# A planned MLP stage that starts four weight tiles earlier and names its buffers

## The chip, the cores and the metric

The kernel runs on one core of a Trainium2 chip, in one launch. The metric is the device time of that launch in microseconds (us), and the median of three runs is taken. TensorE (PE) multiplies matrices; its weight loads (PEld) are listed apart. VectorE (DVE) and ScalarE (ACT) do element-wise work, GpSimd (POOL) a little more of it and the transfers that it issues itself, and SyncE (SP) issues the weight loads from the chip's main memory.

## The reference

A two-layer transformer trunk in fp32, for 256 tokens of width 2048. Each layer adds to the residual stream an attention block (12 main heads and 4 heads that look at 256 memory tokens) and then an MLP:

```python
def sq_relu_mlp(h, g, w_in, w_out):
    return jnp.square(jax.nn.relu(rms_norm(h, g) @ w_in)) @ w_out

def reference(...):
    h = x
    for layer in range(DEPTH):
        ...
        h = h + jnp.concatenate([y_main, y_mem], axis=-1) @ w_o[layer]
        h = h + sq_relu_mlp(h, norm_mlp[layer], w_mlp_in[layer], w_mlp_out[layer])
    return h
```

The MLP's hidden width is 8192, so each layer has two weight matrices of 2048 x 8192. They are most of the work, and all that the change is about lies in or around them.

## The kernel before, in words

**Arithmetic.** Every fp32 weight is split into two parts of the type fp32r: `hi`, a rounded copy, and `lo`, what the rounding lost. A *unit* is one weight block of 128 x 1024. SP loads it (512 KB), ACT casts it to `hi`, DVE subtracts to make `lo`. A product takes hi x hi, hi x lo and lo x hi.

**The up half.** An up tile (`U`, one of 64 per layer) is 128 hidden features for all 256 tokens. It takes two units: 16 matmuls of 512 columns (hi weights against both parts of the activations) and 16 of 256 columns (lo weights). ACT then copies the low half of the bank (`low`), DVE adds the halves (`up`), DVE multiplies `relu` by the token norm (`ri_mlp`, made by `inverse_root`), ACT squares, and the result is split into `hid`. `after_up` lists these operations.

**The down half.** The hidden width is cut into four chunks (`c`) of 16 up tiles. For each chunk the output is done in two halves (`n`). A step `S` is a Strassen-like step with seven products instead of eight: 21 matmuls of 512 columns, from two loads. DVE makes four sums of weight blocks (512 columns each), and ACT and DVE split four units out of the two loads. For each pair of up tiles `block_ops` makes the sums of activations that such a step needs. Steps `A` and `B` are plain products of 12 matmuls. Sums of a chunk leave over POOL's queue to main memory, with an add on the way for later chunks, and come back in the last chunk.

**The order.** `mlp_steps` gives TensorE's order: two tiles done by halves (`H`), pairs of tiles (`T`), single tiles (`U`), then turns of `U` and `S`, and `A`, `B` at a group's end. The `H` and `T` steps run in the plain way: `weights()` prepares at most four units ahead in the pools `raw` (6 buffers), `hi` (4) and `lo` (5), and side work such as `inverse_root` or `finish` is run a given number of *slots* (half a pair of tiles, say) later. In the kernel before the plain way covers tiles 0 to 7, and `up` runs `after_up` at once for tiles 4 to 7 and at fixed slots for tiles 0 to 3.

From tile 8 on (L1450 and after) each engine's order is written out by a planner, `in_turn` (L106). It keeps a clock per engine with fixed costs (`CAST`, `SUM`, `WIDE`), a list of free 128 x 1024 buffers and counts of smaller tiles, and starts a job when its inputs are told and its buffers free. Here the pool `g4` (8 of 9 buffers) joins the 15 of the plain way, so 23 in all, and any of them may hold a load, a `hi` or a `lo`. TensorE, POOL and SP take their jobs in the order given; ACT and DVE take the first of 160 by due time (`key`) that can start. A load starts only if `RESERVE` buffers stay free beside its own. The resulting order is kept by every engine. In the kernel before, the planner chooses a kind and a number, but the tile is then asked of the pool by its kind alone (`slot_tile`, L1450), and the pool gives whichever of its buffers it takes.

The clock of the planner begins at zero for all engines when the `H` and `T` steps have been written.

**After the plan.** The last output tiles come from plain code: four more units are loaded within the plan (`tail_units`), the stored sums are merged (`merged`, `merge_first`), turned by transposes (`turned`), and in the last layer the last four tiles go through `down` and `last_tile`, where GpSimd adds the residual, and are stored.

Everything outside the MLP (projections, attention, output projection) uses the plain way. The pool `g4` holds the heads there, also with buffers that the pool picks.

Of the kernel before, what the change touches and what calls it, by code (L numbers as in the profile page):

```python
# [10 lines left out]
F32 = mybir.dt.float32  # L11
# [28 lines left out]
COPIES, SPARE, HORIZON, SUMS, FROM, LATE, RESERVE, URGENT = 4, 8, 12000, 4800, 5, -7, 3, 3000  # L40
# [51 lines left out]
SOON = 200  # L92


class Job:


    def __init__(self, engine, cost, emit, key, after=(), take=0, give=(), get=(), free=(), adds=False, kinds="g4 raw hi lo"):
# [4 lines left out]
        self.slots, self.tiles, self.kinds = [], [], kinds.split()  # L103


def in_turn(jobs, slots, counts, reserve=RESERVE):  # L106
# [5 lines left out]
    ready = {e: 0 for e in queues}  # L112
# [7 lines left out]
    def fits(job, now):  # L120
        kinds = job.kinds
        if job.engine != "POOL" and (q := queues["POOL"]) and q[0].take and ripe(q[0], now):
            kinds = [x for x in kinds if x != "g4"]
        return [x for x in slots if x[0] in kinds]

    def can(job, now):
# [4 lines left out]
        if job.take and len(fits(job, now)) < job.take + (  # L131
            reserve if job.engine == "SP" else 0
# [4 lines left out]
    while events:  # L137
# [6 lines left out]
        while again:  # L144
            again = False
            for e, queue in queues.items():
# [10 lines left out]
                queue.remove(job)  # L157
# [7 lines left out]
                for _ in range(job.take):  # L165
                    job.slots.append(fits(job, now)[0])
                    slots.remove(job.slots[-1])
# [13 lines left out]
    return order  # L181
# [51 lines left out]
def trunk(  # L233
# [20 lines left out]
    raws = ctx.enter_context(tc.tile_pool(name="raws", bufs=6))  # L254
    his = ctx.enter_context(tc.tile_pool(name="his", bufs=4))
    los = ctx.enter_context(tc.tile_pool(name="los", bufs=5))
    acts = ctx.enter_context(tc.tile_pool(name="acts", bufs=2))
    grp = ctx.enter_context(tc.tile_pool(name="grp", bufs=9))
# [46 lines left out]

    def prepare_pair(load, split):
# [7 lines left out]
                raws.tile([P, 1024], F32, name=f"raw{n}", tag="raw"),  # L314
                his.tile([P, 1024], F32R, name=f"hi{n}", tag="hi"),
                los.tile([P, 1024], F32R, name=f"lo{n}", tag="lo"),
# [15 lines left out]
    def prepare_seven(i, seven):  # L332

        if seven.step == 0:
            seven.raw = []
            for n, ap in enumerate(seven.sides):
                raw = raws.tile([P, 1024], F32, name=f"raw{i}_{n}", tag="raw")
                nc.sync.dma_start(raw[:].rearrange("p (o x) -> p o x", o=4), ap)
                seven.raw.append(raw[:].rearrange("p (o k n) -> p k o n", o=4, k=2))
        left, right = seven.raw  # L340
        b11, b21, b12, b22 = left[:, 0], left[:, 1], right[:, 0], right[:, 1]
        hi = his.tile([P, 1024], F32R, name=f"hi{i}", tag="hi")
        lo = los.tile([P, 1024], F32R, name=f"lo{i}", tag="lo")
        hi4 = hi[:].rearrange("p (k o n) -> p k o n", o=4, k=2)
        lo4 = lo[:].rearrange("p (k o n) -> p k o n", o=4, k=2)
        src = left if seven.step in (0, 3) else right
        if seven.step == 1:
            src, hi4, lo4 = b22, hi4[:, 0], lo4[:, 0]
        elif seven.step == 2:
            nc.vector.tensor_tensor(b22, b22, b12, op=ALU.subtract)  # L350
# [1718 lines left out]
```

## Time and profile before

| what | value |
|---|---|
| runs of the kernel before | 2185.88 us median of 3 (2182.7 to 2189.06) |
| the profiled execution | 2179.71 us, span 2177.9 us, granted clock 0.998 |
| PE busy | 2144.5 us, 98% of the span |
| DVE busy | 1803.9 us, 83% |
| ACT busy | 1308.2 us, 60% |
| POOL busy | 259.7 us, 12% |
| MLP of the first layer, from tile 8 to the end of the plan | about 480 to 1080 us of the span |
| MLP of the second layer, the same | about 1520 to 2120 us |

The profile page gives the busy time of each engine, the span in 40 slices, and the chain of work that ended last. Views of the trace give, for a stretch of the span, each engine's busy time (so idle time is the length less the busy time), the single instructions in order of time with the idle time before them, and the waits. A matmul of 512 columns is listed with some 390 ns, but the next one starts some 227 ns after it: they overlap, and a short stall hides in part in that overlap.

### The profile page before, as it was taken

What the parts mean: (1) busy time and instruction counts of PE and PEld (TensorE: products, weight loads), DVE (VectorE), ACT (ScalarE), POOL (GpSimd) and SP (SyncE); (2) the same over time, 40 slices, a digit from 0 to 9 for tenths busy, and PEclk for the clock granted to TensorE, in tenths of its full rate; (3) what the DMA queues carried; (4) which work ended last, traced back from release to release, by engine and by line L of the source; (5) the groups of instructions that cost most, each with busy time, mean ns of one, the idle gap of its engine ahead of it and who ended that gap; (6) DMA issues with size and microseconds to landing.
All of it is one profiled execution on the core that took longest, in us unless ns stands there. A gap on an engine that the chain in (4) does not pass through costs nothing.

```text
span 2177.9 us, 30420 instructions
## 1 busy us (share of the span) xinstructions
PE 2144.5 (98%) x10966; PEld 1827.2 (84%) x10966; DVE 1803.9 (83%) x2745; ACT 1308.2 (60%) x1968; POOL 259.7 (12%) x307
## 2 busy tenths in 40 slices
PE   9999999999999999999999999999999999999998
PEld 8888888887888888888878888888788888888887
DVE  7778885679999899999785556567999989899985
ACT  7644545556766666666445447555766666676652
POOL 0110112610000000001050112361000000000100
PEclk9999999999999999999999999999999999999999
DMA  9655556675767768769666564467576776886973
GB/s 328 214 162 187 167 182 206 211 245 155 239 210 243 202 196 243 229 199 314 216 188 211 186 191 129 140 214 232 169 231 191 251 212 199 250 233 202 289 245 114
DMA packets 225415, 458.71 MB, mean 211 GB/s; under 512 B 14576, under 2 KB 145648, under 8 KB 225264
## 3 DMA queue, kind: packets, MB, share of 16 engines
q1 hardware_dynamic: 212592, 410.63, 59.7%
q0 software_dynamic: 12096, 44.05, 7.3%
q10 hardware_dynamic: 576, 2.10, 0.3%
q8 instruction: 86, 1.41, 0.3%
q14 instruction: 65, 0.53, 0.1%
HBM read 424.21 MB, written 32.51 MB: 210 GB/s over the span
## 4 chain that ended last, share of the span: by engine, by line
PE 77%; DVE 14%; DMA 5%; issue 3%; ACT 1%; SPq 0%; DVEq 0%; ACTq 0%
PE acc L194 73%; DVE g4s L194 4%; DVE raws L194 2%; DVE los L194 2%; DVE his L194 2%; DMA his<-in_w_down 2%; DMA raws<-in_w_down 1%; PE accs L194 1%; PE yp L194 1%; DVE up L194 1%; DMA los<-in_w_down 1%; DMA g4s<-in_w_down 1%; PE tp L194 1%; PE s L194 1%; PE z L194 1%
## 5 line engine op out<-in xcount | busy, mean ns | idle before, releaser
L304 DVE TENSOR_TENSOR lo<-raw,hi 128x1024 fp32r<-128x1024 f32 (+1 forms) x308 | 382.7, 1251 | 180.1 <-ACT hi L301 153.0
L301 ACT CAST hi<-raw 128x1024 fp32r<-128x1024 f32 (+2 forms) x308 | 318.8, 1039 | 274.2 <-PE acc L194 228.0
L194 PE MATMUL acc<-hi,xg 128*128 128x512 f32 x640 | 208.4, 398 | 0.0
L194 PE MATMUL acc<-mlpx,g4s 128*128 128x256 f32 (+1 forms) x1024 | 190.1, 333 | 0.0
L194 PE MATMUL acc<-mlpx,raws 128*128 128x512 f32 (+1 forms) x960 | 183.2, 336 | 2.0 <-DVE up L194 2.0
L194 PEld LDWEIGHTS acc<-mlpx,g4s 128*128 128x128 f32 x1024 | 161.4, 190 | 21.4
L194 PE MATMUL acc<-g4s,hid 128*128 128x512 f32 x504 | 173.9, 392 | 1.4 <-DVE hid L194 1.1
L194 PEld LDWEIGHTS acc<-mlpx,raws 128*128 128x128 f32 x960 | 153.3, 189 | 24.3 <-DVE up L194 3.2
L194 PE MATMUL acc<-raws,hid 128*128 128x512 f32 x430 | 150.8, 394 | 2.2 <-DVE hid L194 1.3
L194 PE MATMUL acc<-mlpx,los 128*128 128x512 f32 (+1 forms) x720 | 146.7, 350 | 0.0
L194 PEld LDWEIGHTS acc<-hi,xg 128*128 128x128 f32 x640 | 120.2, 188 | 24.7
L194 PE MATMUL acc<-mlpx,his 128*128 128x256 f32 (+1 forms) x752 | 137.6, 328 | 2.6 <-DVE up L194 2.6
L194 PEld LDWEIGHTS acc<-mlpx,los 128*128 128x128 f32 x720 | 120.1, 190 | 18.9
L194 PE MATMUL acc<-los,hid 128*128 128x512 f32 x358 | 129.9, 395 | 4.6 <-DVE los L194 4.4
L194 PEld LDWEIGHTS acc<-mlpx,his 128*128 128x128 f32 x752 | 116.8, 190 | 18.2 <-DVE up L194 3.7
L194 POOL DMA_DIRECT2D e<-copy x24 | 18.2, 760 | 946.2 <-ACT copy L194 942.8
L194 PE MATMUL acc<-lo,xg 128*128 128x512 f32 x320 | 124.8, 390 | 0.6 <-DVE lo L304 0.6
L194 PE MATMUL acc<-y,hi 128*128 128x512 f32 x512 | 119.9, 391 | 0.0
L194 PE MATMUL acc<-his,hid 128*128 128x512 f32 x334 | 115.9, 397 | 0.0
L194 PEld LDWEIGHTS acc<-g4s,hid 128*128 128x128 f32 x504 | 94.0, 188 | 20.8 <-DVE hid L194 2.0
L194 PEld LDWEIGHTS acc<-y,hi 128*128 128x128 f32 x512 | 95.0, 188 | 19.1
L194 ACT ACTIVATE up<-up 128x256 f32<-128x256 f32 x112 | 46.8, 417 | 91.1 <-DVE up L194 90.6
(351 smaller groups left out, 4910.8 us busy)
## 6 DMA issues: line engine op xcount, KB each, us to landing
raw<-in_w_in SPq DMA_DIRECT2D x80, 512.0 KB, 4.1
g4s<-in_w_up SPq DMA_DIRECT2D x76, 512.0 KB, 9.1
g4s<-in_w_down SPq DMA_DIRECT2D x75, 512.0 KB, 8.7
los<-in_w_down SPq DMA_DIRECT2D x72, 512.0 KB, 7.8
raw<-in_w_o SPq DMA_DIRECT2D x64, 512.0 KB, 4.1
raws<-in_w_up SPq DMA_DIRECT2D x58, 512.0 KB, 9.0
raws<-in_w_down SPq DMA_DIRECT2D x53, 512.0 KB, 9.1
los<-in_w_up SPq DMA_DIRECT2D x50, 512.0 KB, 6.7
```

The costliest lines, as they stand in the source:

```text
L194: return self._tc.keep_in_program_order(fn(*args, **kwargs))
L301: nc.scalar.copy(hi[:, :n], raw[:, :n])
L304: nc.vector.tensor_tensor(lo, raw, hi.bitcast(F32), op=ALU.subtract)
```

## The change

The plan starts after one pair step instead of three, so it holds up tiles 4 to 8 and the `after_up` work of tiles 0 to 3 too. Each of the 23 buffers is a tile tag of its own with one buffer, and a job writes exactly the buffer that the planner took; the same is done for the heads in `g4` and for the plain units, which go round in order. `RESERVE` goes from 3 to 4 and counts all free buffers, ACT and DVE are taken to be 1500 ns busy when the plan starts, and the four units loaded for after the plan take one `raw`, one `hi` and one `lo` buffer each instead of any of the three. `inverse_root` starts one slot earlier. In the last layer DVE makes the residual adds of output tiles 14 and 15, which GpSimd made before. The last two pieces of the memory tokens are loaded in program order. A branch for seven-product units in the plain way, which nothing used, is removed.

```diff
+PLANNED = 4
-COPIES, SPARE, HORIZON, SUMS, FROM, LATE, RESERVE, URGENT = 4, 8, 12000, 4800, 5, -7, 3, 3000
+COPIES, SPARE, HORIZON, SUMS, FROM, LATE, RESERVE, URGENT, EARLY = 4, 8, 12000, 4800, 5, -7, 4, 3000, 1500
...
-SOON = 200
+SOON, BACKLOG = 200, 1500
...
 def mlp_steps(l):
     steps = [(0, 0, "H", 0)]
-    steps += [(0, 0, "T", f) for f in range(FIRST_UP, ALONE - 1, 2)]
-    steps += [(0, 0, "U", f) for f in range(ALONE - ALONE % 2, ALONE)]
+    steps += [(0, 0, "T", f) for f in range(FIRST_UP, PLANNED, 2)]
+    steps += [(0, 0, "U", f) for f in range(PLANNED, ALONE)]
...
-    ready = {e: 0 for e in queues}
+    ready = {e: BACKLOG if e in OVERLAP else 0 for e in queues}
...
     def fits(job, now):
-        kinds = job.kinds
-        if job.engine != "POOL" and (q := queues["POOL"]) and q[0].take and ripe(q[0], now):
-            kinds = [x for x in kinds if x != "g4"]
-        return [x for x in slots if x[0] in kinds]
+        queue = queues["POOL"]
+        kept = job.engine != "POOL" and queue and queue[0].take and ripe(queue[0], now)
+        found = []
+        for kinds in job.take:
+            slot_ = next(
+                (x for x in slots if x[0] in kinds and x not in found and not (kept and x[0] == "g4")), None
+            )
+            if slot_ is None:
+                return None
+            found.append(slot_)
+        return found
...
-        if job.take and len(fits(job, now)) < job.take + (
-            reserve if job.engine == "SP" else 0
+        if job.take and (
+            fits(job, now) is None or job.engine == "SP" and len(slots) < len(job.take) + reserve
         ):
...
+    pools = {"raw": raws, "hi": his, "lo": los, "g4": grp}
+    turns = {"raw": deque(range(6)), "hi": deque(range(4)), "lo": deque(range(5))}
+
+    def buffer(kind, m, dtype, name):
+        return pools[kind].tile([P, 1024], dtype, name=name, tag=f"{kind}{m}")
+
+    def next_of(kind, dtype, name):
+        turns[kind].rotate(-1)
+        return buffer(kind, turns[kind][-1], dtype, name)
...
-    def heads4(name):
-        return grp.tile([P, 1024], F32, name=name, tag="g4")
+    def heads4(name, m):
+        return buffer("g4", m, F32, name)
...
     def mlp(l, xg_, sq, h, done):
-        start_side(delayed(inverse_root(sq, f"mlp{l}"), 4))
+        start_side(delayed(inverse_root(sq, f"mlp{l}"), 3))
...
         def up(c, f, bank):
-            early = c == 0 and f < 4
-            add_up(c, f, bank, low_part(bank), early)
-            if early:
-                later(lambda: finish(c, f), began + 11 + f - clock["slot"])
-            else:
-                finish(c, f)
-
+            add_up(c, f, bank, low_part(bank), True)
...
-                job.tiles.append(pools[kind].tile([P, 1024], dtype, name=f"{kind}s{l}_{m}", tag=kind))
+                job.tiles.append(buffer(kind, m, dtype, f"{kind}s{l}_{m}"))
...
+        for f in range(PLANNED):
+            ready_at[0, f] = chain(
+                after_up(0, f), EARLY * f + 1500, None, ready_at[0, f - 1] if f % 2 else ()
+            )
+            if f % 2:
+                held[0, f // 2] = [x for job in ready_at[0, f] for x in job.get if x in ("wide", "bias")]
...
         for m in range(AHEAD + 1):
-            tail_units.append(flat_unit(at, begins[-1] + 1500 * m, "raw hi lo"))
+            tail_units.append(flat_unit(at, begins[-1] + 1500 * m, (("raw",), ("hi",), ("lo",))))
...
-            nc.gpsimd.tensor_tensor(h(o), h(o), t[:], op=ALU.add)
+            (nc.vector if l == 1 and o >= KT - 2 else nc.gpsimd).tensor_tensor(h(o), h(o), t[:], op=ALU.add)
             done(o)
 
         def down_early(o, bank):
             low = low_part(bank)
-            nc.gpsimd.tensor_tensor(low[:], low[:], h(o), op=ALU.add)
+            nc.vector.tensor_tensor(low[:], low[:], h(o), op=ALU.add)
             nc.vector.tensor_tensor(h(o), bank[:, :T], low[:], op=ALU.add)
...
-    qm = heads4("qm0")
+    qm = heads4("qm0", 8)
...
-        q_, k_, v_ = heads4(f"q{i}"), heads4(f"k{i}"), heads4(f"v{i}")
+        q_, k_, v_ = (heads4(f"{x}{i}", m) for x, m in zip("qkv", ((0, 1, 2), (3, 6, 7), (0, 1, 2))[i]))
```

More of the change, by code (lines that the diff above doesn't have):

```diff
@@ L91, with __init__ @@
 LANDS, MOVES, ADDS = 3400, 1690, 2600
-SOON = 200
+SOON, BACKLOG = 200, 1500
 class Job:
-    def __init__(self, engine, cost, emit, key, after=(), take=0, give=(), get=(), free=(), adds=False, kinds="g4 raw hi lo"):
+    def __init__(self, engine, cost, emit, key, after=(), take=(), give=(), get=(), free=(), adds=False):
         self.engine, self.cost, self.emit, self.key = engine, cost, emit, key
@@ L164, in in_turn @@
                     counts[c] -= 1
-                for _ in range(job.take):
-                    job.slots.append(fits(job, now)[0])
-                    slots.remove(job.slots[-1])
+                job.slots = fits(job, now)
+                for x in job.slots:
+                    slots.remove(x)
+                queue.remove(job)
                 if e in ("SP", "POOL"):
@@ L313, in prepare_pair @@
                 stream[n],
-                raws.tile([P, 1024], F32, name=f"raw{n}", tag="raw"),
-                his.tile([P, 1024], F32R, name=f"hi{n}", tag="hi"),
-                los.tile([P, 1024], F32R, name=f"lo{n}", tag="lo"),
+                next_of("raw", F32, f"raw{n}"),
+                next_of("hi", F32R, f"hi{n}"),
+                next_of("lo", F32R, f"lo{n}"),
             )
@@ L330, in prepare_pair @@
         prepared.extend((hi, lo) for _, _, hi, lo in units)
[L332 to L350, printed above, removed]
-            nc.vector.tensor_tensor(b12, b12, b11, op=ALU.subtract)
-            nc.vector.tensor_tensor(b11, b22, b11, op=ALU.add)
-            nc.vector.tensor_tensor(b21, b21, b11, op=ALU.subtract)
-        nc.scalar.copy(hi4, src)
-        nc.vector.tensor_tensor(lo4, src, hi4.bitcast(F32), op=ALU.subtract)
-        seven.step += 1
-        prepared.append((hi, lo))
     def prepare():
@@ L1030, in later @@
         start_side(side())
-    mem_c = [heads4(f"memc{c}") for c in range(4)]
+    mem_c = [heads4(f"memc{c}", c) for c in range(4)]
     def mem(kt):
@@ L1445, in mlp, with __init__ @@
         stay = []
+        class Held:
+            def __init__(self, slots):
+                self.slots = slots
         units = {}
         first_unit = state["next"]
-        pools = {"raw": raws, "hi": his, "lo": los, "g4": grp}
+        ANY = ("g4", "raw", "hi", "lo")
         def slot_tile(job, n, dtype=F32R):
@@ L1492, in lo_ap @@
                 return slot_tile(hi, 1)[:]
-            load = add_job("SP", 0, fetch, key, take=1, kinds=kinds)
+            load = add_job("SP", 0, fetch, key, take=kinds[:1])
             hi = add_job(
-                "ACT", CAST[1024], lambda: nc.scalar.copy(shaped(hi_ap()), raw()), key - 2600, [load], take=2, kinds=kinds
+                "ACT", CAST[1024], lambda: nc.scalar.copy(shaped(hi_ap()), raw()), key - 2600, [load], take=kinds[1:]
             )
@@ L1604, in mlp @@
         last_pe, bring = None, []
-        alone = min(SEVEN[l][0], ALONE // 2)
-        held = {(0, m): ["wide", "bias"] for m in range(alone)}
+        held = {}
         merge = merged(1)
@@ L1708, in mlp @@
                     continue
[L1709 to L1712 removed]
+                job = add_job(
+                    "POOL", 0, lambda: None, begin, [last_pe, landed[id(what[0]), what[1]]], take=[("g4",)],
+                )
+                job.emit = lambda what=what, job=job: bring_sum(*what, job.slots[0][1])
+                returned[id(what[0]), what[1]] = job
             if kind == "U":
```

96 lines of the change are left out of this document (45 added, 51 removed).

## The prediction

> **What bounds the kernel now.** I read the page, then a table of stretches, then single instructions where PE stood still. The page's first rows and its chain of waits:
>
> ```profile
> span 2177.9 us, 30420 instructions
> PE 2144.5 (98%) x10966; PEld 1827.2 (84%) x10966; DVE 1803.9 (83%) x2745; ACT 1308.2 (60%) x1968; POOL 259.7 (12%) x307
> PE 77%; DVE 14%; DMA 5%; issue 3%; ACT 1%; SPq 0%; DVEq 0%; ACTq 0%
> ```
>
> PE idles for 33.4 us in all, so no reordering can be worth much more than 1.5%. The chain leaves PE for DVE in 14% of the span; the table of stretches shows where. Its columns are length, then busy time of PE, PEld, DVE, ACT and POOL, granted clock, DMA share, GB/s. The first eight rows are the first layer's MLP, the others the second's.
>
> ```profile
> 458.00:480.00 22.00, 22.00 (x131) 19.57 (x130) 17.54 (x37) 14.51 (x27) 0.00 (x0) 1.00 0.72 234
> 480.00:493.00 13.00, 13.00 (x74) 11.40 (x73) 12.09 (x28) 8.40 (x18) 0.00 (x0) 1.00 0.99 346
> 493.00:565.00 72.00, 68.54 (x340) 56.33 (x339) 71.66 (x108) 50.82 (x76) 1.15 (x2) 1.00 0.56 164
> 565.00:735.00 170.00, 170.00 (x869) 145.67 (x870) 164.44 (x243) 115.68 (x174) 4.95 (x8) 1.00 0.70 228
> 735.00:770.00 35.00, 31.79 (x161) 26.63 (x160) 29.30 (x42) 21.01 (x30) 1.72 (x2) 0.99 0.82 226
> 850.00:906.00 56.00, 54.86 (x277) 45.91 (x276) 55.62 (x83) 38.05 (x57) 1.71 (x2) 1.00 0.68 218
> 906.00:1038.00 132.00, 132.00 (x680) 113.02 (x679) 123.99 (x182) 86.67 (x129) 8.99 (x13) 1.00 0.83 254
> 1038.00:1080.00 42.00, 41.01 (x204) 34.56 (x202) 31.11 (x41) 21.76 (x30) 2.69 (x5) 1.00 0.62 197
> 1519.60:1532.60 13.00, 13.00 (x74) 11.39 (x73) 12.09 (x28) 8.40 (x18) 0.00 (x0) 1.00 0.97 345
> 1532.60:1604.60 72.00, 68.57 (x340) 56.34 (x338) 71.66 (x108) 50.72 (x75) 1.15 (x2) 1.00 0.55 163
> 1774.00:1810.00 36.00, 32.81 (x166) 27.47 (x165) 30.29 (x44) 21.42 (x31) 1.74 (x2) 1.00 0.83 228
> 1890.00:1945.60 55.60, 54.41 (x272) 44.85 (x272) 55.19 (x81) 38.77 (x58) 1.73 (x2) 1.00 0.69 213
> 2077.60:2119.60 42.00, 40.98 (x204) 34.62 (x203) 33.59 (x44) 24.81 (x35) 2.69 (x5) 1.00 0.70 221
> ```
>
> Right after the plan's start (about 480) DVE is full: 71.66 of 72 us, while the DMA moves only 164 GB/s. PE waits 3.46 us there. Just before, in 458 to 480, DVE idles 4.46 us and in 480 to 493 another 0.91: 5.37 us of DVE time lie unused ahead of a stretch that lacks it. The second layer repeats it to 0.03 us. So the order of work, not its amount, costs PE time here. PE's instructions show what one such wait costs:
>
> ```profile
> 493.73 0.39 PE L194 MATMUL acc<-his,hid 128*128 128x512 f32 x1
> 495.64 0.50 PE L194 MATMUL acc<-los,hid 128*128 128x512 f32 x1 [1.52 <-DVE los L194]
> 495.97 0.39 PE L194 MATMUL acc<-his,hid 128*128 128x512 f32 x1
> 496.20 0.40 PE L194 MATMUL acc<-his,s_w 128*128 128x512 f32 x1
> ```
>
> Undisturbed starts are 0.23 us apart (495.97, 496.20); here they are 1.91 apart, so 1.68 us are lost where the row shows 1.52 idle. Each wait hides 0.16 us in the overlap. I count seven in 493 to 565, so the loss is 3.46 + 7 x 0.16 = 4.6 us per layer.
>
> **The change, part by part.**
>
> *Plan from the fifth tile.* PE issues the same matmuls: a planned tile has 32, as half a pair has. What moves is when ACT, DVE and SP may work ahead. Why DVE idled before 480:
>
> ```profile
> 412.73 55.64 SPq L380 DMA_DIRECT2D raw<-in_w_up  x20
> 468.42 1.23 SPq L194 DMA_DIRECT2D g4s<-in_w_down  x2
> L304 DVE TENSOR_TENSOR lo<-raw,hi 128x1024 fp32r<-128x1024 f32 x10 | 12.2, 1222 | 2.7 <-ACT hi L301 2.1 <-PE acc L194 0.6
> L1248 DVE TENSOR_TENSOR hid<-up,hid 128x256 fp32r<-128x256 f32 x8 | 3.4, 419 | 1.7 <-ACT hid L1245 1.7
> ```
>
> SP issued plain loads until 468, and the two DVE groups of 458 to 493 waited 4.4 us for ACT and for PE to free one of four `hi` buffers. With the plan, loads into `g4` can follow the twelfth unit of the stage instead of the twentieth, and DVE has 23 buffers and a choice of jobs. If all 5.37 us are used, DVE enters the full stretch with more lead than the 4.6 us it lacks, and the whole loss goes: -4.6 per layer. If the lead can't be held (buffers full, or wrong jobs taken first), only the first wait goes: -1.7. The capacity row speaks for the upper end; since the last waits lie 70 us later and the lead must last through them, I take 4.2: **-8.4 us** for both layers. The work of tiles 0 to 3 that is now planned is the same instructions on the same engines: 0.
>
> *Inverse root one slot earlier.* The rows that bound it:
>
> ```profile
> 441.90 0.75 POOL L611 TENSOR_TENSOR mlpsq<-mlpsq,sq 128x256 f32<-128x256 f32 x1
> 445.35 3.04 PE L194 MATMUL acc<-mlpx,lo 128*128 128x256 f32 x24
> 448.23 0.50 PE L194 MATMUL stat<-neg_ones,mlpsq 128*128 128x2 f32 x4
> 461.50 0.61 PE L194 MATMUL inv<-dg,neg_ones 128*128 128x128 f32 x4
> ```
>
> `stat` moves ahead of the last 16 of those 24 matmuls, some 1.9 us, to about 446.3. Its input is complete at 442.65, so PE doesn't wait: 0. Without that cover it would cost up to 1 us.
>
> *Last two output tiles.* The end of the kernel:
>
> ```profile
> 2169.13 2.15 PE L194 MATMUL acc<-hid,lo 128*128 128x256 f32 x16
> 2169.41 0.69 DVE L1178 TENSOR_TENSOR hb<-tp,hb 128x512 f32<-128x512 f32 x1 [3.13 <-PE tp L194]
> 2169.42 0.74 POOL L1855 TENSOR_TENSOR low<-low,hb 128x256 f32<-128x256 f32 x1 [2.92 <-ACT low L578]
> 2170.20 0.42 DVE L1856 TENSOR_TENSOR hb<-acc,low 128x256 f32<-128x256 f32 x1
> 2171.31 0.42 DVE L1859 TENSOR_TENSOR hb<-acc,hb 128x256 f32<-128x256 f32 x1 [0.69 <-PE acc L194]
> ```
>
> POOL's 0.74 us become one more 0.42 us on DVE: 2169.41 + 0.69 + 0.42 + 0.42 = 2170.94, and the last add still waits for PE's end at 2171.28. The last store starts when it did. So 0, with 0.34 us of cover; without it at most +0.4.
>
> *Units loaded for after the plan.* They must now take all four `hi` buffers, whichever planned unit holds them. PE lost 0.99 and 1.02 us in the rows 1038 to 1080 and 2077.6 to 2119.6. Nothing shows the new wait; its bounds are 0 and one such loss more per layer. I take 0.3 each, near the lower end since DVE idles 10.9 us in the first of these rows: **+0.6 us**.
>
> *Named buffers, one more in reserve, and an order planned anew in the rest.* From 565 on PE idles 3.21, 1.14 and 0.99 us in the first layer's rows and 3.19, 1.19 and 1.02 in the second's: 10.7 us is the most it can gain. At worst the new order loses as much: +10.7. Nearest to what is planned anew are the rows 565 to 735 and 906 to 1038, 302 us without any PE idle: there the order has slack, so I take 0 and keep both ends.
>
> Sum: -8.4 + 0.6 = -7.8 us. The profiled execution took 2179.71 (its span and 1.8 us around it); it becomes 2171.9. The median of the runs shown is 6.2 us above that execution, so the same step from it gives **2178 us**.
>
> **The rivals.**
>
> *Later stalls go too.* The wait that costs most after 565 begins at a late load:
>
> ```profile
> 731.72 1.08 SPq L194 DMA_DIRECT2D los<-in_w_down  x1
> 752.02 0.62 ACT L194 CAST los<-los 128x512 fp32r<-128x512 f32 x1 [6.26 <-PE acc L194]
> 769.53 0.75 PE L194 MATMUL acc<-his,s_w 128*128 128x512 f32 x1 [1.89 <-DVE his L194]
> 769.60:773.00 3.40, 3.40 (x8) 2.69 (x9) 3.26 (x7) 1.46 (x2) 0.00 (x0) 0.50 0.39 144
> los<-in_w_down SPq DMA_DIRECT2D x36, 512.0 KB, 7.7
> ```
>
> ACT stands for 6.26 us and starts 20.3 us after the load's issue, where the median load lands in 7.7 us; I read the wait as the load's, not PE's. One wait follows on PE with a granted clock of 0.50 for 3.40 us, which costs 1.7 us more. If an exact buffer for each job and fewer loads in the air remove 60% of the 10.7 us and this clock dip, the sum is -7.8 - 6.4 - 1.7 = -15.9: 2170 us. Against it: naming a buffer moves no byte faster. [...]
>
> *The gain is handed back.* The first stretch is cleared, but PE then reaches the late loads at 735 sooner and waits there for what it saved, as those loads follow the DMA's own pace. Left is what the loads allow, about the first wait in one layer: -1.7, 2184 us. For it: 6.26 us of ACT's wait that DVE's lead doesn't touch. Against: 170 us without PE idle lie between, and loads are issued as PE frees buffers, so they move with it.
>
> *Slower: held-back loads land late.* A `U` and an `S` take 15 buffers; 16 x 0.23 + 16 x 0.12 + 21 x 0.23 make that 10.3 us, so a load that waits for one more free buffer is issued 0.69 us later. If it lands as much later, about five waits per layer after 565 grow by it (6.9 us in all), the two stretches per layer without idle get one each (2.8), and two clock dips come (3.4); half of the early gain stays (-4.2): +8.9, 2195 us. It decides from 8.4 / 14 = 0.6 us of lateness per wait. For it: the late load above. [...]
>
> **How the numbers follow.** A measurement of this kernel can tell about 0.3%, 6.6 us, from no change. Forecast 0.45 (2178; its own range 2173 to 2183), later stalls too 0.18, handed back 0.19, slower 0.18. Faster by more than 6.6 us (below 2179.3): 0.29 of the forecast's 0.45 and the second's 0.18, 0.47. Within: 0.16 of the forecast, 0.17 of the handed back and 0.02 of the slower, 0.35. Slower: the other 0.16 and 0.02, 0.18. The range goes from 2166, a little past the second case, to 2193, which leaves out the worse part of the slower one.
>
> **What would show it.** Right: in the rows that answer to 493 to 565 and 1532.6 to 1604.6 PE idles under 0.6 us each and DVE stays full; the stretch before has DVE busy over 95%; loads into `g4` begin before 450 (the twelfth of the twenty plain loads lies near 412.73 + 0.6 x 55.64 = 446). Handed back: that stretch clear, but more than 3.2 us of PE idle around 735. Slower: more ACT waits that end at a landing, new PE waits in 565 to 735 or 906 to 1038. Wrong at the root: PE still waits for `lo` right after 490 though DVE was free before, which would mean that buffers or loads, not the plan's start, set it.

## The result and the profile after

The changed kernel takes 2156.49 us (median of 4 runs, 2152.92 to 2158.2); the kernel before, run beside it on the same chip, 2184.29 (2181.91 to 2189.06). The ratio is 0.9868, its 95% interval 0.9845 to 0.9891: 27.8 us are gone. The prediction was 2178, range 2166 to 2193. The direction was right, the size not: three and a half times as much was won, and the time lies below the range.

The page of the changed kernel, its first rows and its chain of waits (2155.2 us, the span and 1.8 us around it):

```profile
span 2153.4 us, 30286 instructions
PE 2137.3 (99%) x10966; PEld 1828.4 (85%) x10966; DVE 1802.8 (84%) x2747; ACT 1308.5 (61%) x1968; POOL 257.7 (12%) x305
PE 88%; DVE 6%; DMA 4%; issue 1%; ACT 1%; ACTq 0%; DVEq 0%
```

PE's idle time falls from 33.4 to 16.1 us, and DVE's share of the chain from 14% to 6%. The table of stretches, in the columns used before; the second layer's stretches are moved by what was won until then:

```profile
458.00:480.00 22.00, 22.00 (x128) 19.41 (x127) 21.47 (x46) 17.66 (x34) 0.00 (x0) 1.00 0.56 178
480.00:493.00 13.00, 13.00 (x77) 11.49 (x76) 12.52 (x23) 9.71 (x17) 0.00 (x0) 1.00 0.06 25
493.00:565.00 72.00, 70.78 (x356) 59.85 (x355) 71.17 (x108) 48.31 (x73) 1.15 (x2) 1.00 0.72 219
735.00:770.00 35.00, 32.13 (x157) 27.04 (x156) 28.08 (x42) 19.77 (x29) 1.34 (x2) 0.95 0.85 252
850.00:906.00 56.00, 56.00 (x286) 47.93 (x285) 55.57 (x82) 40.10 (x61) 1.89 (x3) 1.00 0.68 209
1038.00:1080.00 42.00, 42.00 (x203) 35.40 (x203) 32.37 (x44) 18.14 (x24) 3.77 (x7) 1.00 0.84 271
1080.00:1130.00 50.00, 46.51 (x220) 38.20 (x219) 44.19 (x52) 24.11 (x32) 25.77 (x26) 1.00 0.68 205
1524.70:1596.70 72.00, 70.52 (x353) 59.30 (x353) 70.74 (x108) 47.66 (x73) 1.14 (x2) 1.00 0.72 222
1763.00:1799.00 36.00, 35.50 (x180) 29.97 (x179) 31.77 (x46) 22.81 (x33) 1.74 (x2) 1.00 0.93 273
2062.00:2104.00 42.00, 41.06 (x204) 34.62 (x203) 32.42 (x42) 21.90 (x31) 3.17 (x6) 1.00 0.76 248
2104.00:2125.00 21.00, 21.00 (x98) 17.35 (x97) 16.91 (x21) 7.39 (x8) 0.00 (x0) 1.00 0.72 231
```

The first row is what the plan's earlier start does: DVE is busy for 21.47 of 22 us where it was for 17.54, and in the third PE idles 1.22 us instead of 3.46. After that nearly every stretch is better; 735 to 770 alone hardly changes (2.87 us of idle time for 3.21, and a granted clock of 0.95 for 0.99).

Busy time hides part of what PE loses, so I also counted from each matmul's start to the next, less the usual distance after a matmul of its kind (227 ns for 512 columns, 120 for 256). Both kernels have the same 10,966 matmuls. Their order differs only from 446 to 480 us, and in the like stretch of the second layer, where tiles are planned that were not before; so from 480 on the start of the same matmul can be compared through the whole span. The change by place in the profiled pair, first and second layer, in us:

| place (time in the kernel before) | first layer | second | both |
|---|---|---|---|
| first stretch of the plan (436 to 669, 1509 to 1717) | -3.7 | -3.2 | -6.9 |
| around the late load (669 to 850, 1717 to 1838) | -0.3 | -2.6 | -2.8 |
| rest of the plan (850 to 1057, 1838 to 2075) | -2.9 | -3.1 | -6.0 |
| end of the plan, stored sums merged (1057 to 1181, 2075 to 2160) | -1.1 | -4.5 | -5.6 |
| last matmul's start to the span's end | | -3.2 | -3.2 |

The sum is -24.5, as the spans say. The other 3.3 us of the medians can't be placed: the profiled execution of before, 2179.71, lies 4.6 us below the median beside which the result is measured. My sum had a gain at the first of the five places alone.

The end of the span needs rows that I hadn't thought of. The last adds in the changed kernel, on DVE and on POOL:

```profile
2138.47 0.74 POOL L1841 TENSOR_TENSOR hb<-hb,dn 128x256 f32<-128x256 f32 x1 [5.12 <-DVE dn L1840]
2150.04 0.42 DVE L1850 TENSOR_TENSOR hb<-acc,hb 128x256 f32<-128x256 f32 x1 [0.58 <-PE acc L202]
```

From DVE's last add to the span's end 3.4 us pass; before it was 6.6 (2171.31 to 2177.9). The reason stands in records that the views leave out, of the kind DRAIN, one at each engine's end. Start and length in us, and the span's end:

```
                     GpSimd drain starts  length  ends      DVE's last add  span ends
before               2169.385             7.731   2177.12   2171.31         2177.9
changed kernel       2138.436             7.729   2146.17   2150.04         2153.4
```

GpSimd's drain starts with its last add and takes 7.7 us. Before, it ran 0.8 us short of the very end of the span; now it is over before DVE's last add begins.

### The profile page after: what moved, and what is told of

Read it like the earlier page. It is cut to its first block, busy times and chain, and to the rows that moved or that the text cites. A ratio compares the mean times of both kernels' runs of the same rounds, so it can differ in the third digit from the quotient of the medians.

```text
span 2153.4 us, 30286 instructions
## 1 busy us (share of the span) xinstructions
PE 2137.3 (99%) x10966; PEld 1828.4 (85%) x10966; DVE 1802.8 (84%) x2747; ACT 1308.5 (61%) x1968; POOL 257.7 (12%) x305
## 4 chain that ended last, share of the span: by engine, by line
PE 88%; DVE 6%; DMA 4%; issue 1%; ACT 1%; ACTq 0%; DVEq 0%
PE acc L202 83%; DMA raws<-in_w_down 2%; DMA g4s<-in_w_up 2%; DVE g4s L202 1%; DVE raws L202 1%; PE accs L202 1%; PE yp L202 1%; PE tp L202 1%; PE s L202 1%; PE z L202 1%; DVE los L202 1%; DVE his L202 1%; DMA sum<-e 0%; DVE lo L364 0%; DVE up L202 0%
## 5 line engine op out<-in xcount | busy, mean ns | idle before, releaser
L312 DVE TENSOR_TENSOR lo<-raw,hi 128x1024 fp32r<-128x1024 f32 (+1 forms) x292 | 363.2, 1253 | 173.4 <-ACT hi L309 147.9
L309 ACT CAST hi<-raw 128x1024 fp32r<-128x1024 f32 (+2 forms) x292 | 301.9, 1038 | 262.8 <-PE acc L202 218.3
L202 PE MATMUL acc<-mlpx,los 128*128 128x512 f32 (+1 forms) x1072 | 205.7, 338 | 0.0
L202 PE MATMUL acc<-mlpx,g4s 128*128 128x256 f32 (+1 forms) x1104 | 199.6, 327 | 0.0
L202 PEld LDWEIGHTS acc<-mlpx,los 128*128 128x128 f32 x1072 | 172.8, 189 | 24.7
L202 PEld LDWEIGHTS acc<-mlpx,g4s 128*128 128x128 f32 x1104 | 171.0, 190 | 21.1
L202 PE MATMUL acc<-g4s,hid 128*128 128x512 f32 x484 | 159.1, 393 | 2.6 <-DVE hid L202 1.3
L202 PE MATMUL acc<-mlpx,his 128*128 128x512 f32 (+1 forms) x624 | 123.4, 341 | 3.4 <-DVE up L202 3.4
L202 ACT COPY low<-acc 128x256 f32<-128x256 f32 x120 | 44.4, 370 | 121.2 <-PE acc L202 120.6
L202 PEld LDWEIGHTS acc<-mlpx,his 128*128 128x128 f32 x624 | 101.1, 190 | 18.5 <-DVE up L202 4.2
```

What stands on the lines that cost most here:

```text
L202: return self._tc.keep_in_program_order(fn(*args, **kwargs))
L309: nc.scalar.copy(hi[:, :n], raw[:, :n])
L312: nc.vector.tensor_tensor(lo, raw, hi.bitcast(F32), op=ALU.subtract)
```

## The experiments

Before the single runs, what they add up to. Medians and ratios are against the kernel before in the same job; the places are those of the table above, from the profiled execution of each against that of before. That execution of before lies below those medians, so the places of a row show 1 to 7 us less gain than its medians do (14.0 of 20.9 for reserve 4 alone). In the five jobs the kernel before took 2182.4 to 2185.1 us; medians from different jobs carry a difference of that size.

A place can also move without any change of the program. The changed kernel and the one with GpSimd's last adds keep the same order on every engine until 2144.9 us, but from 669 to 850 the one has -0.3 and the other -4.4, and in the like place of the second layer -2.6 and -0.3. So a few us at the late load, read from one execution, show little.

| kernel | median us | ratio (95%) | first | late load | rest | end of plan | last store |
|---|---|---|---|---|---|---|---|
| changed | 2156.5 | 0.9868 (0.9845 to 0.9891) | -6.9 | -2.8 | -6.0 | -5.6 | -3.2 |
| before + early start alone | 2166.3 | 0.9917 (0.9902 to 0.9932) | -6.1 | -6.3 | +2.4 | -3.0 | 0.0 |
| before + reserve 4 alone | 2164.3 | 0.9906 (0.9892 to 0.9921) | +0.4 | -7.8 | -2.6 | -4.3 | +0.1 |
| before + names and the rule for the four units | 2197.4 | 1.0067 (1.0052 to 1.0082) | 0.0 | +3.4 | +1.3 | +12.8 | 0.0 |
| changed, GpSimd's last adds | 2159.3 | 0.9886 (0.9871 to 0.9901) | -7.1 | -4.7 | -4.6 | -4.4 | 0.0 |
| changed, reserve 3 | 2176.7 | 0.9971 (0.9960 to 0.9983) | -8.6 | -2.0 | +1.8 | +6.9 | -3.2 |
| changed, start at tile 8 | 2168.0 | 0.9924 (0.9908 to 0.9941) | +0.4 | +0.6 | -5.5 | -2.9 | -3.2 |
| changed, no names | 2151.2 | 0.9851 (0.9836 to 0.9866) | -8.0 | -7.9 | -5.3 | -4.4 | -3.2 |

### Undoing one part of the changed kernel

**GpSimd's last adds.** The two places of the last tiles go back:

```diff
-            (nc.vector if l == 1 and o >= KT - 2 else nc.gpsimd).tensor_tensor(h(o), h(o), t[:], op=ALU.add)
+            nc.gpsimd.tensor_tensor(h(o), h(o), t[:], op=ALU.add)
...
-            nc.vector.tensor_tensor(low[:], low[:], h(o), op=ALU.add)
+            nc.gpsimd.tensor_tensor(low[:], low[:], h(o), op=ALU.add)
```

> The changed kernel with GpSimd making the residual adds of output tiles 14 and 15 again; nothing else differs. Drain theory: the launch ends only when GpSimd has drained, 7 us after its last operation, so the span runs on for about 6.2 us after DVE's last add instead of 2.9: 3.2 us slower, 2159.7 against 2156.5. Rival (the adds themselves were on the path): the span after DVE's last add stays at 2.9 us and that add itself ends about 0.3 us later, 2156.8.

2159.34 us, 2.9 more. The intervals of the two ratios overlap, so what settles it is the end of the span. From the last matmul's start to the span's end it is 6.9 us again, as before, against 3.7. The drain runs from 2149.005 for 7.731 us, and the span ends 0.8 us after it.

**Reserve three.**

```diff
-COPIES, SPARE, HORIZON, SUMS, FROM, LATE, RESERVE, URGENT, EARLY = 4, 8, 12000, 4800, 5, -7, 4, 3000, 1500
+COPIES, SPARE, HORIZON, SUMS, FROM, LATE, RESERVE, URGENT, EARLY = 4, 8, 12000, 4800, 5, -7, 3, 3000, 1500
```

> The changed kernel with RESERVE back at 3. If the free buffers are what cleared the later stalls (at 905, 1038, 1800, 1940 and 2124 us of the kernel before), those come back, some 4 to 10 us, 2161 to 2166, and the first stretch after 480 stays clear. If the buffers' names cleared them, nothing moves by more than 1.5 us.

2176.74 us: 20.3 us more than the changed kernel, from one number. The first stretch keeps its whole gain; 12.5 us are lost at the ends of the plans (+6.9 against -5.6). Its instructions at the second layer's end:

```profile
2097.13 0.53 POOL L202 DMA_DIRECT2D sum<-d  x1 [6.46 <-DMA raws<-in_w_down]
2108.86 0.53 POOL L202 DMA_DIRECT2D sum<-e  x1 [11.20 <-PE acc L202]
2117.32 0.69 DVE L202 TENSOR_TENSOR sum<-sum,sum 128x512 f32<-128x512 f32 x1 [2.72 <-DMA sum<-e]
2122.14 0.47 PE L202 MATMUL tp<-ident,sum 128*128 128x128 f32 x1 [5.43 <-DVE sum L202]
2124.92 0.90 PE L202 MATMUL tp<-ident,sum 128*128 128x128 f32 x3 [2.31 <-DVE sum L202]
```

The last of the eight stored sums is fetched at 2108.86, after POOL waited 11.20 us for PE. It may go into a `g4` buffer only, and a split had taken the one that had come free; it held it until PE had used it. DVE's merge waits for the landing, PE's transposes for the merge.

**No names.** The pools of the kernel before (`raws` with 6 buffers, and so on) and one tag per kind:

```diff
-        return pools[kind].tile([P, 1024], dtype, name=name, tag=f"{kind}{m}")
+        return pools[kind].tile([P, 1024], dtype, name=name, tag=kind)
```

> The changed kernel with the pools giving whichever buffer they take: six raw, four hi, five lo and nine g4 buffers under one tag each, as before; planner and start as changed. If the names cleared the later stalls, 6 to 11 us come back, 2162 to 2167, spread over waits of ACT, DVE and SP for a buffer that another had freed later. If the new order did it, under 2 us.

2151.22 us, 5.3 less than the changed kernel, though the intervals of the two ratios overlap. In these two executions nearly all of it lies around the late load (-7.9 against -2.8); the kernel with GpSimd's last adds, named too, has -4.7 there.

**Start at tile 8.** `PLANNED` 8 instead of 4, with the slots of tiles 0 to 3 and of `inverse_root` as before:

```diff
-PLANNED = 4
+PLANNED = 8
```

> The changed kernel with the plan starting at tile 8 again (tiles 4 to 7 in pairs, their follow-up work at once, that of tiles 0 to 3 at fixed slots, inverse root a slot later); names, reserve, backlog and tail as changed. If the early start gives only the first stretch, PE idles there 3 to 3.5 us per layer again and the time is 6 to 9 us up, 2163 to 2165. If the lead it gives also clears later stalls, 12 to 18 us up, 2169 to 2174, with stalls beyond 700 us of the span back too.

2167.97 us. The first stretch loses all that was won (+0.4 against before). The place of the late load, some 250 us further on, has +0.6 against -2.8; how much of that is the start's, one execution can't tell.

### One part alone on the kernel before

The sum of the prices (11.5, 20.3, 2.9, less 5.3 for the names) is 29.4, near the whole; but where they act overlaps, so I put each part alone on the kernel before.

```diff
-... RESERVE, URGENT = 4, 8, 12000, 4800, 5, -7, 3, 3000
+... RESERVE, URGENT = 4, 8, 12000, 4800, 5, -7, 4, 3000
```

> The kernel before with one constant changed: loads leave four buffers free, not three. Theory A (the parts simply add; taking the reserve out of the changed kernel cost 20.3 us): 2184.3 - 20.3 = 2164. Theory B (the reserve only mends what the earlier start spoils): no change, 2181 to 2186. Theory C (the two parts share their gain; the changed kernel with the late start took 2168.0, and the last tiles on GpSimd cost 2.9 more): 2171, with PE still idle some 3.5 us in the stretch that answers to 493 to 565, and no stall over 2 us at the end of the second layer's plan.

2164.26 us beside 2185.14: the first theory's number, 20.9 us for one constant.

The early start alone is the changed kernel with nearly everything else undone; the rule for the four units loaded for after the plan and the way the reserve is counted stay as changed:

```diff
-COPIES, SPARE, HORIZON, SUMS, FROM, LATE, RESERVE, URGENT, EARLY = 4, 8, 12000, 4800, 5, -7, 4, 3000, 1500
+COPIES, SPARE, HORIZON, SUMS, FROM, LATE, RESERVE, URGENT, EARLY = 4, 8, 12000, 4800, 5, -7, 3, 3000, 1500
-SOON, BACKLOG = 200, 1500
+SOON, BACKLOG = 200, 0
-        return pools[kind].tile([P, 1024], dtype, name=name, tag=f"{kind}{m}")
+        return pools[kind].tile([P, 1024], dtype, name=name, tag=kind)
...
```

> The kernel before with the plan from the fifth tile alone: reserve three, no backlog at the plan's start, pools that pick any buffer of a kind, GpSimd adding in all tiles. My prediction's own step for this part (-8.4 and +0.6): 2184.3 - 7.8 = 2176.5. Theory A (parts add; undoing the start cost 11.5): 2172.8. Theory C (the start without the reserve hands later what it wins first: 2176.7 of the changed kernel with reserve three, and 2.9 for the last tiles): 2177 to 2180; the first stretch of each layer clear (3.7 and 3.2 us won), and a stall of 5 us or more at the end of the second layer's plan, where the last stored sum comes back late.

2166.32 us: 18.8 us, more than any theory gave. The two kernels, first reserve four and then the early start; 493, 735 and 1774 begin the first stretch and the two late loads:

```profile
493.00:565.00 72.00, 68.76 (x341) 56.50 (x339) 71.59 (x107) 51.21 (x76) 1.15 (x2) 1.00 0.54 163
735.00:770.00 35.00, 35.00 (x177) 29.59 (x176) 31.01 (x45) 22.66 (x33) 1.72 (x2) 1.00 0.96 276
1774.00:1810.00 36.00, 36.00 (x190) 31.00 (x190) 32.26 (x47) 23.65 (x33) 0.51 (x1) 1.00 0.83 246
```

```profile
493.00:565.00 72.00, 70.42 (x353) 59.19 (x352) 71.36 (x107) 49.37 (x74) 1.15 (x2) 1.00 0.64 195
735.00:770.00 35.00, 34.57 (x177) 29.28 (x176) 32.31 (x46) 22.69 (x32) 1.42 (x2) 1.00 0.78 211
1774.00:1810.00 36.00, 36.00 (x185) 30.82 (x185) 34.04 (x53) 22.54 (x34) 0.00 (x0) 1.00 0.71 199
```

Only the start clears the first stretch. Either of them clears the stalls of 3.2 us around the late loads and the late merge at the second layer's end; what both remove can be won once. That is why 18.8 and 20.9 and 2.9 don't add up: the kernel that has all three and no names is 31.2 us below before, not 42.6.

The names without the rest (but with the rule for the four units loaded for after the plan) are the changed kernel with `PLANNED` 8, `RESERVE` 3, `BACKLOG` 0 and GpSimd's last adds, the tags left as they are:

```diff
-PLANNED = 4
+PLANNED = 8
-SOON, BACKLOG = 200, 1500
+SOON, BACKLOG = 200, 0
...
```

> The kernel before with the named buffers alone: plan from the ninth tile, three left free, no backlog, GpSimd adding in the last tiles. Theory 'names cost' (three pairs of kernels that differ in the names, or in them and the last tiles, show 5.3, 7.7 and 6.8 us): 2184 + 5 to 8 = 2189 to 2192. Rival 'names cost only where the reserve is four, by where the loads then fall beside the sums': 2182 to 2186. My prediction's step: 0.

2197.41 us, 15.0 *more* than before. It is the largest loss of the study, and 12.8 us of it lie at the two plan ends. POOL and PE in this kernel, first layer:

```profile
1078.37 0.54 POOL L202 DMA_DIRECT2D sum<-e  x1 [14.55 <-PE acc L202]
1105.01 0.90 PE L202 MATMUL tp<-ident,sum 128*128 128x128 f32 x3 [6.09 <-DVE sum L1186]
```

and the same fetch in the kernel before:

```profile
1062.20 0.54 POOL L194 DMA_DIRECT2D sum<-e  x1 [1.50 <-PE acc L194]
```

Within the plan every engine has the same order in both until the last loads before this fetch, at some 1060 us. Before, the pool handed out its own next `g4` buffer, which happened to be free; by name, the fetch waits for the one in the plan, 14.55 us. Not all of that is the name's. Each kernel's planner, on its own clock, sets this fetch at 590.2 us here and at 585.6 in the kernel before, since the rule for the four units changes which buffers are free; in the second layer at 590.2 against 592.9. So, by estimate, 4.5 us of the wait in the first layer go back to the rule. No run has the names without it, so how the 15.0 us divide between the two stays open.

### Is it the last return?

If a split that takes the last `g4` buffer is the cause, keeping that buffer must cure it. One rule more in the planner's `fits`:

```diff
+        last = sum(1 for x in queue if x.take) <= 2
-        kept = job.engine != "POOL" and queue and queue[0].take and ripe(queue[0], now)
+        kept = job.engine != "POOL" and queue and queue[0].take and (last or ripe(queue[0], now))
```

> The changed kernel with reserve three, and one rule more in the plan: from the seventh of the eight stored sums on, a free g4 buffer is kept for the sum that comes back. The plan's order is the same up to there; the last return is planned 8.1 us earlier. Theory 'late return' (with reserve three the last return waits for a g4 buffer that a split has taken, and that makes the 9.4 us lost at the end of the second layer's plan and 1.2 in the first's): 2176.7 - 9 to 10.6 = 2166 to 2168, no PE idle over 2 us on tp<-ident,sum in 2110 to 2125. Rival 'late anyway' (DVE's merges are late because DVE is behind, whatever the return does): 2174 to 2177, the same stall. Either way the 10 us lost between 906 and 1080 and in the second layer's like stretches stay.

2163.08 us, 13.7 less than without the rule. POOL's last fetches, and then the stretch around them:

```profile
2088.51 0.53 POOL L203 DMA_DIRECT2D sum<-d  x1 [1.74 <-PE acc L203]
2093.23 0.53 POOL L203 DMA_DIRECT2D sum<-e  x1 [4.19 <-DVE los L203]
```

```profile
2090.00:2130.00 40.00, 40.00 (x190) 33.39 (x189) 30.68 (x39) 16.31 (x20) 1.04 (x2) 1.00 0.80 260
```

With reserve three and no such rule that stretch has 32.27 us of PE:

```profile
2090.00:2130.00 40.00, 32.27 (x141) 26.40 (x140) 24.79 (x32) 14.83 (x21) 2.10 (x4) 0.87 0.70 225
```

The end of the plans goes from +6.9 to -6.0, all other places stay within 1.2. So the late return is shown as the cause of 13 of the 20 us. The rest of the plan stays at +0.7 where reserve four has -6.0. There the loads land late: with reserve three SP issued seven loads in 891 to 898 while POOL's sums went out, and the last of them took 21.2 us to land. That is read from one trace and wasn't tried by itself.

> The kernel before with one rule more in its plan: from the seventh of the eight stored sums on, a free g4 buffer is kept for the sum that comes back. Its last return is planned 3.6 us earlier in the first layer and 10.9 us earlier in the second; all other orders stay. Theory 'late return' (the 4.0 us that PE loses on the last sums at the end of the second layer's plan, and part of the 4.7 in the first, come from a return that waits for a g4 buffer): 3.2 to 4.5 us gone in the second layer, up to 2 in the first: 2184.6 - 3.2 to 6.5 = 2178 to 2181.4. Rival (that stall is DVE's own lag there, which another order of the whole plan removed in the other kernels): 2183 to 2187.

The same rule in the kernel before brings little: 2181.75 us, ratio 0.9986 (0.9976 to 0.9995). The second layer's end gains 4.0 us, as expected; the first loses 4.4. There the new order puts the add that frees a bank of PE's (`sum<-acc,sum`) behind the merge's own sums on DVE, and PE waits for it:

```profile
1081.81 2.74 DVE L196 TENSOR_TENSOR sum<-sum,sum 128x512 f32<-128x512 f32 x4
1085.79 0.68 DVE L196 TENSOR_TENSOR sum<-acc,sum 128x512 f32<-128x512 f32 x1
1086.53 0.57 PE L196 MATMUL acc<-los,hid 128*128 128x512 f32 x1 [4.58 <-DVE sum L196]
```

In the kernel before two of these adds run first:

```profile
1079.23 1.28 DVE L194 TENSOR_TENSOR sum<-acc,sum 128x512 f32<-128x512 f32 x2
1080.43 2.74 DVE L194 TENSOR_TENSOR sum<-sum,sum 128x512 f32<-128x512 f32 x4
```

So an earlier fetch is a gain only where the order behind it holds.

With reserve four, the rule on the changed kernel without names:

> The changed kernel without names (pools pick any buffer of a kind, 2151.2 so far), with the same rule for the last two returns: the last return is planned 2.8 us earlier. Theory 'late return': the 1.9 us that the unnamed kernel loses on the last sums in each layer shrink, 2147.5 to 2150. Rival (with reserve four the return is early enough, the wait there is DVE's own): 2150 to 2152.5, no change.

2148.14 us, ratio 0.9833 (0.9818 to 0.9847), the fastest kernel of the study: 8.4 us below the changed one, 3.1 below the one without the rule, with -7.2 against -4.4 at the ends of the plans. The same with `RESERVE` 5 instead of 4:

> The unnamed kernel with the rule for the last two returns (2148.1) and five buffers left free, not four. Theory 'more reserve, fewer late loads and waiting splits': some of the 9 us that PE still loses in the two plans goes, 2144 to 2147. Theory 'the order is a draw; reserve four happens to be good and the loads get shorter leads': 2149 to 2158.

2155.2 us, ratio 0.9877 (0.9861 to 0.9894). Reserve five is 7 us worse than four: the rest of the plan gains nothing (0.0 against -5.1). "More is better" falls; four is a good draw.

### Why names cost, and the late load

The rule in the changed kernel as it is, names kept:

> The changed kernel with the same rule; beside the unnamed kernel with this rule (2148.1) it differs only in that each buffer is the one that the plan names. Theory 'names cost' (a stall of some 3 us and a clock dip at 735 to 770, which the profiles of two named kernels have and no unnamed one): 2152 to 2156, with that stall in its profile. Theory 'names are nothing': 2147 to 2150, no stall there. Against the changed kernel itself (2156.5) the rule should bring 0 to 3, as its last return is planned 2.8 us earlier.

2155.81 us, 0.9877 (0.9862 to 0.9892): with names the same order is 7.7 us slower than without, and its four runs spread over 4.7 us instead of 1.2. Most of what can be seen lies at the late load and the first layer's end (-5.5 and +1.1 against -8.4 and -1.4). A third pair agrees: the changed kernel with the start at tile 8 has the plan of the kernel with reserve four alone up to the last four units, and names; it has +0.6 at the late load where that has -7.8. In the changed kernel:

```profile
723.47 0.34 SPq L202 DMA_DIRECT2D g4s<-in_w_up  x1
725.73 0.38 SPq L202 DMA_DIRECT2D raws<-in_w_down  x1
726.38 0.90 POOL L202 DMA_DIRECT2D e<-copy  x1 [69.80 <-ACT copy L202]
741.77 0.62 ACT L202 CAST g4s<-raws 128x512 fp32r<-128x512 f32 x1 [6.01 <-DMA raws<-in_w_down]
746.10 2.53 PE L202 MATMUL acc<-mlpx,his 128*128 128x512 f32 x8 [2.87 <-DVE up L202]
```

and the same issues in the unnamed kernel with the rule:

```profile
722.14 0.34 SPq L203 DMA_DIRECT2D g4s<-in_w_up  x1
725.12 0.46 SPq L203 DMA_DIRECT2D raws<-in_w_down  x1
726.21 0.90 POOL L203 DMA_DIRECT2D e<-copy  x1 [69.80 <-ACT copy L203]
```

By name SP's first load here is issued 1.33 us later, and so the burst behind it starts later; POOL's accumulating copies start at nearly the same time in both (0.17 us apart). So `raws<-in_w_down` is issued 0.65 us ahead of the first copy by name (call that its lead), and 1.09 us ahead without names. The last columns of the transfers' view (KB, us from issue to landing) for the load `raws<-in_w_down`, in the changed kernel and in the unnamed one:

```profile
raws<-in_w_down SPq DMA_DIRECT2D x1, 512.0 KB, 16.0
```

```profile
raws<-in_w_down SPq DMA_DIRECT2D x1, 512.0 KB, 9.1
```

Issued 0.6 us earlier, it lands 7.5 us earlier. But that is one pair of landings. In the kernel with GpSimd's last adds, which has the changed kernel's order and names up to here, the load is issued 0.64 us ahead of the first copy in the first layer and 0.63 in the second, and takes 9.9 and 15.9 us; only the second layer has the stall:

```profile
735.00:770.00 35.00, 34.70 (x182) 29.57 (x181) 30.78 (x45) 22.22 (x32) 1.72 (x2) 1.00 0.88 257
1763.00:1799.00 36.00, 33.25 (x170) 28.13 (x169) 30.64 (x45) 22.07 (x32) 1.74 (x2) 1.00 0.88 261
```

Over both layers of four named kernels with reserve four and the early start (changed, GpSimd's last adds, the rule for returns, no backlog), the load has a lead of 0.63 to 0.65 us and takes 16.0, 13.6, 9.9, 15.9, 14.8, 13.8, 16.2 and 9.4 us: late (13.6 us or more) in six of eight. In the two unnamed kernels the lead is 1.09 to 1.10 us, and it takes 9.3, 9.2, 9.1 and 8.8 us: late in none of four. In these eight cases the landing with the shorter lead was a draw (9.4 to 16.2 us), which fits the wider spread of the runs.

To see whether the copies make it late, I left them out:

```diff
-                else:
+                elif c != 1:
                     nc.gpsimd.dma_start(
                         out=homes[k][:], in_=g.copies[id(homes), k][:], accum_op=ALU.add
                     )
```

> The changed kernel without the eight accumulating copies per layer that GpSimd sends to DRAM for the second of the four chunks (those at 726 to 735 and 808 to 828 in the first layer); so the stored sums lack that chunk. Nothing else changes in any engine's order. Theory 'load behind the sums' (the load that PE waits for at 742.84 is issued 0.65 us ahead of the first of these copies and lands 16.0 us later, while in the unnamed kernel it is issued 0.6 us earlier and lands after 9.1): that load lands within 10 us, the stall of 3 us and the clock dip in 735 to 770 go, and the like in 1775: 2156.5 - 4 to 7 = 2149.5 to 2152.5. Rival (the names make SP wait for the wrong buffer, with or without the copies): the stall stays, 2155 to 2158.

2152.45 us. Its ratio, 0.9863 (0.9846 to 0.9879), can't be told from the changed kernel's. In its trace the load, issued at 725.48, lands after 9.7 us, in the second layer after 10.0, and both stalls are gone though the buffers are still named:

```profile
735.00:770.00 35.00, 35.00 (x186) 30.26 (x185) 32.63 (x47) 22.79 (x33) 0.00 (x0) 1.00 0.59 188
1774.00:1810.00 36.00, 36.00 (x191) 31.04 (x190) 33.78 (x56) 23.51 (x36) 0.00 (x0) 1.00 0.55 175
```

As 9.4 and 9.9 us also came with the copies in place, these two landings alone show little. The loads behind them show more: a later one of SP's (`g4s<-in_w_down`, issued at 735.06 in the changed kernel) takes 15.5 us, and 14.8 to 15.7 in the three other named kernels; without the copies, issued at 735.21, it takes 5.1. So the copies made that load some 10 us late. That the names cost time here because they cut the lead of one load over the copies fits all the landings, but no run changed the lead by itself.

### Two small parts

```diff
-SOON, BACKLOG = 200, 1500
+SOON, BACKLOG = 200, 0
...
-            (nc.vector if l == 1 and o >= KT - 2 else nc.gpsimd).tensor_tensor(h(o), h(o), t[:], op=ALU.add)
+            nc.gpsimd.tensor_tensor(h(o), h(o), t[:], op=ALU.add)
```

> The changed kernel with two edits 1600 us apart, each read at its own place: ACT and DVE free at the plan's start (no backlog of 1500 ns), and GpSimd again doing one of the two adds that had gone to DVE, that of the last tile but one. Backlog, theory 'order at the start': PE loses about 1 us more in each first stretch, as in the kernel with the start alone; rival: nothing. Tail, theory 'GpSimd's drain' (7.7 us from the start of its last add to its end, which with this add at about 2144.9 is over as the last store is): 0 to 0.7 us from the last matmul to the end more than the 5.5 of the changed kernel's profile; rival 'each add on GpSimd costs its share': 1.5 us more. In all 2156 to 2160.

2160.21 us. The backlog does nothing where it was meant to: the first stretch has -6.8 against -6.9. GpSimd's one add, started at 2150.10, has its drain over at 2157.79, and the end from the last matmul grows by 0.2 us: the drain counts, not the add. The median is still 3.7 us above the changed kernel's, though the intervals of the two ratios overlap. In the profiled execution the loss lies at the end of the second layer's plan (-0.9 against -4.5) and in the rest (-4.6 against -6.0); whether the new order or the execution makes it is open.

## Why the prediction was wrong

**Plan from the fifth tile, -8.4: right where I put it.** The first stretches gain 6.9 us in the changed kernel and 8.0 without names. What I said would show it came: DVE at 98% before 480, `stat` at 446.35 where I had 446.3, loads into `g4` from 444.20 on. Two waits of 0.6 to 0.7 us remain per layer, so PE idles 1.22 and 1.48 us, not under 0.6. Counted from start to start, the kernel before lost 5.6 us in each of these stretches, not the 4.6 of my sum: one wait's 0.16 us was too little for all seven. What the step missed is that its gain reaches further: put on the kernel before, the early start also clears the late loads and the second layer's late merge (-6.3 and -3.0), as it gives the rest of the plan a new order too.

**Inverse root, 0: right.** No wait ahead of `stat`.

**Last two output tiles, 0 (at most +0.4): wrong by 3.2 us, a second term that failed.** I compared POOL's 0.74 us with DVE's 0.42 up to the last add, and took it that the last store ends the span. The last add's row (2171.31 + 0.42) and the span (2177.9) had 6.2 us between them in sight; I didn't ask what fills them. It is GpSimd's drain.

**Units loaded for after the plan, +0.6: not seen.** PE idles 0.00 and 0.94 us in the rows that answer to 1038 to 1080 and 2077.6 to 2119.6, where it idled 0.99 and 1.02. With reserve three this rule may have a part in the 15.0 us that it costs together with the names.

**Named buffers, one more in reserve, a new order: 0, bounds -10.7 to +10.7. This is the step that failed,** in three ways.

*The bound was too small.* I added up PE's idle time in six rows, 10.7 us, and called it the most that could be won. The rows left out the merge behind each plan:

```profile
1080.00:1130.00 50.00, 45.81 (x211) 37.17 (x210) 45.13 (x55) 21.05 (x27) 22.81 (x23) 1.00 0.69 202
2119.60:2135.00 15.40, 12.74 (x54) 10.14 (x53) 9.70 (x13) 3.83 (x5) 0.00 (x0) 0.89 0.71 228
```

That is 4.2 and 2.7 us more. And idle time understates a loss, as I had worked out myself for the first stretch (1.52 idle, 1.68 lost) and not applied here; a clock dip is busy time altogether (PE is busy for all 3.40 us from 769.60, at a granted clock of 0.50). Counted from start to start, PE lost 28.4 us after 565 in the two plans and merges. The changed kernel loses 14.1 there: 14.3 us won, more than my whole bound.

*The value was taken from the wrong place.* I chose 0 because 302 us without PE idle lie "nearest to what is planned anew". Those stretches can't gain; the stalls can, and both other orders that were tried without names remove most of them: the early start and reserve four, each without the other, take 6.3 and 7.8 us at the late loads.

*Three edits under one sum.* "Edits with one answer go together" hid that they have opposite signs: reserve four brings 20.9 us alone, the names with the four units' rule cost 15.0. With reserve four the names cost less (5.3 and 7.7 us in two pairs, of which the second alone is clear of noise): the last return waits less, and what is left lies mostly at the late load.

**The rivals.** "Later stalls go too" had the mechanism and the wrong size: -15.9 was its end, because it was a share of the same 10.7 us and had no merge and no drain in it. I also argued against it that "naming a buffer moves no byte faster". The names did harm here; what helped was the reserve, which I didn't weigh apart. "Gain handed back" is what the changed kernel's profile shows in 735 to 770 of the first layer (a wait of 2.87 us, then a granted clock of 0.53 for 3.40 us), but another execution of the same order (GpSimd's last adds) has no such wait there. "Held-back loads land late" has the sign wrong: holding loads back leaves buffers for splits and returns. Reserve five, though, is a first step on its road.

## What to carry to other kernels

Bound what a new order may win by the time lost from start to start over every stretch that it touches, ends included, and price edits of opposite sign apart. Ask of the last instruction and of the end of the span what fills the time between them. In a planned order, look for the job that only one kind of buffer can serve: here one fetch per layer decided 13 us. Before one execution's gain at one place is put down to an edit, look at that place in another kernel that has the same order.

## What the hardware showed that I had not expected

GpSimd's drain at the kernel's end takes 7.72 to 7.73 us from the start of its last add in the four kernels of this question (before, the changed one, and the two with adds given back). The span ended 0.8 us after it where it came last, and 3.4 us after the start of DVE's last add in the changed kernel, where it didn't; so, by estimate, an add on GpSimd later than 5 us ahead of that one (7.7 + 0.8 - 3.4) is paid at the end. The one at 5.5 us cost 0.2.

One load, issued 0.63 to 0.65 us ahead of the first of GpSimd's accumulating copies, took between 9.4 and 16.2 us to land in eight cases; issued 1.09 to 1.10 us ahead, between 8.8 and 9.3 in four. The latency of this load was no constant (6.8 us apart for leads that differ by 0.02), and an estimate by which a load "lands as much later" as it is issued later, as mine did, is far off for it.

The granted clock fell to 0.53 after a wait of 2.87 us on PE in the changed kernel:

```profile
747.80:751.20 3.40, 3.40 (x9) 2.63 (x9) 3.40 (x4) 2.00 (x2) 0.00 (x0) 0.53 0.78 261
```

In the kernel without the copies, where the wait was gone, it was 1.00 over the whole of 735 to 770. What makes it fall, no run shows.
